# A residual stream with channels on the partitions, and full-height scores, in a two-layer trunk

## The chip, the cores and the metric

One core of a Trainium2 chip runs the whole program. The metric is device time in microseconds, the median of the runs shown. The engines are PE (TensorE, with its weight loads PEld), DVE (VectorE), ACT (ScalarE), POOL (GpSimd) and SP (SyncE, whose queue issues nearly all DMAs).

## The reference

512 tokens of 1024 channels go through two layers. Each layer normalises, projects, runs two groups of heads, gates them, projects back and adds to the residual x; then a per-layer embedding is added through a sigmoid gate. All arithmetic is float32.

```python
for i in range(2):
    h = rms_norm(x, norm_gain[i])
    y = even_layer(h) if i == 0 else odd_layer(h)
    x = x + y
    gate = sigmoid(rms_norm(x, ple_norm_gain[i]) @ w_ple_gate[i])
    x = x + (p[i] @ w_ple_proj[i]) * gate

def odd_layer(h):                      # layer 1
    cq, ck, cv, cg, dq, dk, dv, dg = split(h @ w_in)
    cq, ck, dq, dk = [rope(rms_norm(z, gain)) for z in ...]   # 8 heads of 64
    oc = dilated_attention(cq, ck, cv)       # head group C, causal patterns
    od = diff_attention(dq, dk, dv, lam)     # D: softmax 1 - lam * softmax 2
    return concat(oc * silu(cg), od * silu(dg)) @ w_out
```

Layer 0 has the same shape with head group A (each query attends to its 128 best keys by an indexer) and B (a window of 128 keys with sinks).

## The kernel before, in words

Tokens come in 4 tiles of 128 (NT), channels in 8 K tiles of 128 (NK). Every operand of a large product is split into a high and a low part in a reduced float32 format (`hilo`: ACT writes the high part, DVE the rest), and a product takes three matmuls, `PASSES = ((0, 0), (0, 1), (1, 0))`. The activations of the running projection lie in `AT`, channels on the partitions, [128, hi/lo, 8 K tiles, 512 tokens].

The residual `X` has tokens on the partitions. `norm` turns it: `turn` does 4 transposes on PE for each token tile and half of the channels and splits the result into AT, while `norm_scale` takes the sum of squares on ACT and a power on POOL, for a scale per token (`rs`). A scale per token is applied at evacuation, where tokens are partitions. Where they are columns (`proj_gate`), `scale_rows` sends the scales through DRAM and back to all partitions.

`proj_tok` computes a projection with tokens on the partitions, for 4 token tiles in 4 banks of PSUM (tag mm): order "kt" walks the K tiles outside, "tok" one bank after the other. `head_evac` scales, rotates and normalises the heads, turns them back with 4 transposes (tag tk), and `put_heads` writes [channels, tokens] in a pair of tiles (high, low). `put_stacked`, used in layer 0, instead stacks high and low parts of one head over 128 partitions by 4 DMAs, so that `scores` needs 2 matmuls for a head. In layer 1, `score_pairs` computes two heads at once in 64-row matmuls, 3 passes each, placed next to one another (`together`). The scores go to banks of tag sk, the attention output to tag ob. `out_half` adds the output projection to X, `ple` does the gate: tanh on ACT with the scale per token, and two DVE passes.

The order is that of a planner. `Program` records all calls (so every row of the profile has the line of the one place that issues them, L278) and `order()` schedules them per engine by a table of prices (`_price`, `LATENCY`) and by numbers (`LEADS`, one row for each kind of part) that move a part forwards or back in rank. The order on each engine is then fixed, SP included: a DMA that waits holds back those behind it. Rings set further waits: raw weights 4 tiles, split weights (w) 8, slots 8, mm banks 4, sk 2, tk 1, ob 1.

PE starts with ten products of zeros while the first loads are under way; x and the weights of the first projection come by K tiles 0, 1, then 2 and 3 of x in one load.

Of the kernel before, what the change touches and what calls it, by code (L numbers as in the profile page):

```python
# [12 lines left out]
F32 = mybir.dt.float32  # L13
# [18 lines left out]
    "att": (-392, -476, -265, 55, 575, -382, 44, 15, -6, -149, -341, -446, -4, -57, 63, -14, 2, 2, -287, 388, 0, 0,  # L32
         -65, 0, 0, -340, 0, -3, -78, 11, -243, 35, 122, -14, 0, -146),
    "ev": (12, 0, -121, 83, 78, -30, 61, -7, 7, 155, 29, 342, -212, 353, -715, 362, 407, -56, 322, -31, 200, 16, -145,
         -150, 0, 30, -1, -7, 53, -154, 6, 182, -674, -420, 817, -28, -108, -22, 70, -40, 70, 33, -1100, -2051, 35,
         822, 12, -44, 0, 0, -2, 0, 0, -147, 0, -27, -283, 17, 0, 12, 205, -6, 199, 0, -12, -29, 1, 69, -144, -2, 0,
         -60, -17, -132, -121, 0, -4, -30, -25, 158, -369, 425, 0, 348, 223, 189, -144, 392, -848, 105, -367, 17,
         -129, -1338, 5, 109, -567, -263, 0, -2347, -61, 293, 0, -2, 0, 1, -4, -10366, 101, 61, -322, 216, 72, 25,
         -1240, 202, 109, 0, 142, 0),
    "idx": (-5, -2, 0),  # L40
    "mm": (15, 0, 153, 0, 10, -336, -84, 2, 8, 4, 0, -30, 30, -5, 88, -12, -304, 0, 41, 13, 136, -25, 206, -141, -135,
         -6, -996, -1930, -2303, -10383),
    "norm": (-3, -2, 0, -170, 60, -38, 0, -13, 142, 15, 0, -227, 0, -49, 15, -1, 0, 0, -396, -7, 21, 0, 0, -1844),
    "rows": (0, 898),
    "ss": (-64, 0, 0, 340, 576, 4, -39, 1269, 0, 0, -74, 119, 196, 55, 333, 112, -4, 45, -250, -182, 70, 0, 0, 1, 14,
         -119, 0, 74, 0, 1, 0, -88),
    "tab": (279, 13, -4, 0, -137, -2),
    "top": (193, -101, -908, -1349, 180, 58, -8, -21, -2, 3, -1659, -1846),
    "w": (-57, 169, 413, -21, 0, -44, -172, 0, 3, 0, -2, 1, -44, 74, -2, -20, -89, 234, 3, 68, -363, 0, 0, -80, -19,
         0, -19, 0, -854, -1336),  # L50
    "x": (2, 0),
    "y": (825, 483, 0, -2, -20, 0, 0, -16, 32, 4, 0, 202, 1, -123, -517, -335),
    None: 62,
# [4 lines left out]
SWITCH = 200  # L58
WHOLE = frozenset(range(512))
PR = 8  # L60
QB = 2
# [18 lines left out]
class Program:  # L80
# [18 lines left out]
    def __init__(self, tc):  # L99
        self.tc = tc  # L100
        for e in self.ENGINES:
            setattr(self, e, _Engine(self, e))
        self.calls, self.cost, self.after, self.rank = [], [], [], []
        self.lead, self.parts = LEADS.get(None, 0), {}
        self.touched, self.users, self.rings, self.bytes, self.groups = {}, {}, {}, {}, {}
        self.mode, self.joined, self.place, self.extra = {}, None, 0, {}
# [23 lines left out]
    def _price(self, engine, method, reads, writes):  # L130
# [22 lines left out]
        return 218 / 128 * n  # L153

    @contextmanager
    def together(self):

        self.joined = []
        yield
        i, = set(self.joined)  # L160
        self.cost[i] /= 2
        self.joined = None

    def add(self, engine, method, args, kw):
        if self.joined:
            i = self.joined[0]
            self.calls[i][1].append((method, args, kw))
        else:
            i = len(self.calls)
            self.calls.append((engine, [(method, args, kw)]))  # L170
            self.rank.append((self.place - self.lead, i))
            self.cost.append(0)
            self.after.append(set())
        self.place += 1
        if self.joined is not None:
            self.joined.append(i)
# [4 lines left out]
        if engine == "tensor":  # L181
            self.mode[i] = reads[0].ap[0][1], writes[0].ap[0][1]
# [43 lines left out]
    def order(self):  # L226
# [17 lines left out]
        dma, mode = 0.0, None  # L244
# [4 lines left out]
        while len(out) < n:  # L249
# [6 lines left out]
            if i in self.mode:  # L256
                t += SWITCH * (mode not in (None, self.mode[i]))
                mode = self.mode[i]
# [23 lines left out]
def tile_trunk(ctx: ExitStack, tc: tile.TileContext, a: dict, out: bass.AP):  # L282
# [38 lines left out]
    for _ in range(10):  # L321
        nc.tensor.matmul(bank, zeros[:, :P], zeros, start=True, stop=True)
# [83 lines left out]
    def proj_tok(pieces_n, evac, tiles=range(NT), order="kt", act=None, swap=0, cut=False, first=False):  # L406
# [5 lines left out]
        def mms(t, i, c0=0, c1=n, passes=range(3)):  # L412
            kt, w2 = pieces[i]
            for c in passes:
                xa, wa = PASSES[c]
                nc.tensor.matmul(banks[t][:, c0:c1], act[kt ^ (4 * swap)][:, xa, t * P:(t + 1) * P], w2[:, wa, c0:c1],
                                 start=(i == 0 and c == 0), stop=(i == last and c == 2))
        if order == "kt":
# [10 lines left out]
            for t in tiles:  # L429
                evacuate(evac, t, banks[t])  # L430
        else:
            for t in tiles:
                halves = ((0, 256), (256, 512)) if cut and t == NT - 1 else ((0, n),)
                for c0, c1 in halves:
                    banks[t] = mm_bank()
                    for i in range(last + 1):
                        mms(t, i, c0, c1)
                    evacuate(evac, t, banks[t], *((c0, c1) if cut else ()))

    @nc.part("mm")  # L440
    def proj_gate(pieces_n, y0, done, rsb):
# [3 lines left out]
        for i, (kt, w2) in enumerate(pieces):  # L445
            for m in range(4):
                for c, (xa, wa) in enumerate(PASSES):
                    nc.tensor.matmul(banks[m], w2[:, wa, m * P:(m + 1) * P], AT[:, xa, kt, :],
# [34 lines left out]
    def norm_scale(t, rs, times=1.0):  # L483
# [5 lines left out]
        if times != 1.0:  # L489
# [640 lines left out]
```

## Time and profile before

| what | us |
|---|---|
| median of 3 runs | 676.76 (676.32 to 677.66) |
| profiled execution, its own time | 677.39 |
| its span, first to last instruction | 675.6 |
| PE busy | 668.0 (99%) |
| DVE busy | 513.7 (76%) |
| ACT busy | 415.4 (61%) |
| POOL busy | 68.7 (10%) |
| mean DMA rate | 110 GB/s |

The mean granted TensorE clock over the span is 1.00. Matmuls overlap in PE, so the length of one is more than what it costs in a row; pace is read from start to start. A tile's name in a row is that of the program without its number: `sk<-ident,slot` is a transpose of the residual, `sk<-slot,slot` a score, `mm<-w,AT` or `mm<-AT,w` a projection (what streams stands first, then what is stationary). A form such as 64*128 64x512 gives the rows and columns of the array that are used, then the shape that streams.

### The profile page before, as it was taken

How to read it: one execution, taken by the hardware profiler on the slowest of the kernel's cores; microseconds unless marked ns; L12 is line 12 of the kernel's file. 1: busy time of each engine (PE TensorE's matmuls, PEld its weight loads, DVE VectorE, ACT ScalarE, POOL GpSimd, SP SyncE). 2: the span in 40 equal slices, each digit the busy share in tenths (PEclk: the TensorE clock that was granted, in tenths of full speed). 3: DMA queues.
4: the chain of work that ended last, by engine and by line, in shares of the span. 5: the costliest groups of instructions: out<-in, count | busy, mean ns of one | idle time of the engine just before them, and what ended most of it. 6: DMA issues, size and time to landing. Idle time of an engine off the chain costs nothing.

```text
span 675.6 us, 10378 instructions
## 1 busy us (share of the span) xinstructions
PE 668.0 (99%) x3494; PEld 543.9 (81%) x3494; DVE 513.7 (76%) x1225; ACT 415.4 (61%) x957; POOL 68.7 (10%) x55
## 2 busy tenths in 40 slices
PE   8999999999999999999999999999999999999997
PEld 5888888888988888887778877777887777888886
DVE  6699999999999646464795298989869698655443
ACT  6765678999889725355554365766637476564341
POOL 0120132000100000000230040003031000100100
PEclk9999999999999999999999999999999999999999
DMA  9855146653131521253353322123213034132222
GB/s 333 299 144 153 63 126 168 183 148 141 48 111 49 185 79 54 71 183 101 87 156 99 94 62 79 48 63 94 86 40 97 29 114 136 48 111 63 93 79 78
DMA packets 49621, 74.23 MB, mean 110 GB/s; under 512 B 5920, under 2 KB 18592, under 8 KB 49312
## 3 DMA queue, kind: packets, MB, share of 16 engines
q1 hardware_dynamic: 49424, 73.56, 35.3%
q8 instruction: 27, 0.44, 0.3%
q14 instruction: 26, 0.21, 0.1%
q10 hardware_dynamic: 144, 0.02, 0.0%
HBM read 61.49 MB, written 6.30 MB: 100 GB/s over the span
## 4 chain that ended last, share of the span: by engine, by line
PE 92%; DMA 3%; DVE 2%; ACT 1%; issue 1%; SPq 0%; DVEq 0%; ACTq 0%
PE mm L278 70%; PE sk L278 8%; PE ob L278 7%; PE tk L278 6%; DMA raw<-in_w_in_odd_dram 2%; DMA slot<-in_xT_dram 1%; DVE t L278 1%; DMA raw<-in_w_out_odd_dram 1%; DVE w L278 1%; ACT w L278 0%; DVE AT L278 0%; ACT t L278 0%; DVE slot L278 0%; SPq L278 0%; DVE tiny L278 0%
## 5 line engine op out<-in xcount | busy, mean ns | idle before, releaser
L278 PE MATMUL mm<-w,AT 128*128 128x512 f32 (+2 forms) x1728 | 433.6, 397 | 1.2 <-ACT w L278 0.6
L278 PEld LDWEIGHTS mm<-w,AT 128*128 128x128 f32 x1728 | 313.4, 188 | 69.6 <-issue 1.6
L278 PE MATMUL mm<-AT,w 128*128 128x512 f32 x384 | 104.9, 404 | 0.0
L278 ACT ACTIVATE w<-raw,gains 128x512 fp32r<-128x512 f32 x96 | 67.7, 722 | 58.8 <-PE mm L278 51.5
L278 DVE SCALAR_TENSOR_TENSOR w<-raw,gains,w 128x512 fp32r<-128x512 f32 x96 | 69.9, 746 | 39.1 <-ACT w L278 38.7
L278 POOL TENSOR_TENSOR tiny<-tiny,mhalf 128x8 f32<-128x8 f32 (+1 forms) x32 | 56.9, 1780 | 351.2 <-DVE tiny L278 351.2
L278 PEld LDWEIGHTS mm<-AT,w 128*128 128x128 f32 x384 | 68.6, 189 | 12.9 <-issue 1.1
L278 ACT ACTIVATE pr<-pr,nm 128x256 f32<-128x256 f32 (+3 forms) x128 | 68.6, 539 | 11.6 <-DVE nm L278 11.3
L278 PE MATMUL sk<-slot,slot 128*128 128x256 f32 (+7 forms) x368 | 64.6, 330 | 0.0
L278 DVE TENSOR_TENSOR w<-raw,w 128x512 fp32r<-128x512 f32 x80 | 53.8, 682 | 14.0 <-ACT w L278 13.6
L278 ACT CAST w<-raw 128x512 fp32r<-128x512 f32 x79 | 47.6, 620 | 22.2 <-PE mm L278 13.4
L278 PEld LDWEIGHTS sk<-slot,slot 64*128 64x128 f32 (+1 forms) x368 | 43.9, 187 | 12.0 <-issue 3.8
L278 PE MATMUL tk<-ident,pr 128*128 128x128 f32 x256 | 43.7, 275 | 0.0
L278 DVE SCALAR_TENSOR_TENSOR t<-t,slot 128x512 f32<-128x512 f32 (+1 forms) x17 | 11.2, 659 | 35.0 <-ACT t L278 35.0
L278 PEld LDWEIGHTS ob<-pt,Ve 128*128 128x128 f32 x272 | 35.1, 191 | 2.7 <-ACT pt L278 1.2
L278 PE MATMUL ob<-pt,Ve 128*128 128x128 f32 x272 | 37.2, 276 | 0.0
L278 PEld LDWEIGHTS tk<-ident,pr 128*128 128x128 f32 x256 | 31.2, 141 | 7.0 <-ACT pt L278 1.5
L278 ACT ACTIVATE t<-mm,rsn 128x512 f32<-128x512 f32 (+1 forms) x17 | 11.0, 662 | 40.0 <-PE mm L278 40.0
L278 DVE TENSOR_TENSOR t<-raww,tab 128x512 f32<-128x512 f32 x48 | 32.4, 684 | 4.0 <-ACT raww L278 3.9
L278 DVE CUSTOM_DVE_ANT_0 pr<-sk,cpack 128x128 f32<-128x128 f32 (+3 forms) x72 | 31.1, 461 | 5.6 <-PE sk L278 5.5
L278 ACT COPY pt<-tk 128x512 f32<-128x512 f32 (+3 forms) x56 | 27.4, 489 | 12.1 <-PE tk L278 8.6
L278 POOL TENSOR_TENSOR rsn<-tiny,mhalf 128x1 f32<-128x1 f32 x16 | 11.3, 710 | 215.6 <-DVE tiny L278 215.5
(100 smaller groups left out, 797.1 us busy)
## 6 DMA issues: line engine op xcount, KB each, us to landing
raw<-in_w_in_odd_dram SPq DMA_DIRECT2D x64, 256.0 KB, 2.8
raw<-in_w_in_even_dram SPq DMA_DIRECT2D x36, 256.0 KB, 3.0
raw<-in_w_ple_gate_dram SPq DMA_DIRECT2D x32, 256.0 KB, 2.6
slot<-in_x_dram SPq DMA_DIRECT2D x16, 256.0 KB, 6.6
raw<-in_w_out_even_dram SPq DMA_DIRECT2D x16, 256.0 KB, 2.8
raw<-in_w_out_odd_dram SPq DMA_DIRECT2D x16, 256.0 KB, 2.6
slot<-qh SPq DMA_DIRECT2D x22, 128.0 KB, 2.4
slot<-ql SPq DMA_DIRECT2D x22, 128.0 KB, 2.5
```

The source lines that it names most:

```text
L278: getattr(getattr(nc, engine), method)(*args, **kw)
```

## The change

The residual X now has channels on the partitions. The residual is loaded from the transposed copy of x that the host passes already, the output projection, the embedding product and the gate swap their stationary and moving operand (`flip`), and the result is written as (channels, tokens) and turned on the host. `norm` has no transposes: `split_x` splits each K tile from SBUF into AT, `add_squares` squares it on ACT and adds the squares up on DVE, `column_scales` sums over the partitions with 4 float32 matmuls against a column of −0.5 and takes one power on POOL, and `scale_rows` makes rows of the scales by 4 transposes and a copy, without DRAM. The gate's evacuation multiplies by these rows on DVE ahead of tanh. Gates and ck take a new order "mix".

For C and D, keys are stacked as in layer 0 (`put_stacked`), and queries go to DRAM (`put_far`) and are fetched for each score by `fetch`, twice high and low over 64 partitions, into a ring of three tiles (`HOMES`). The scores are 128-row matmuls, 2 for each head. The first loads of x come as K tiles 0, 1, 2, 3 one at a time with the weights in turn, and nine products of zeros stand in place of ten. The planner loses its price for changes of form, and its numbers LEADS are new, all of them.

```diff
-    "norm": (-3, -2, 0, -170, 60, -38, 0, -13, 142, 15, 0, -227, 0, -49, 15, -1, 0, 0, -396, -7, 21, 0, 0, -1844),
+    "norm": (-7, -21, -1139, -422, 0, 163, 0, -1317, 0, -65, -255, 143, -554, 273, -6, 8, -797, 9, 343, 0, 45, 356,
...
-SWITCH = 200
...
+HOMES = ("ve", "acc12", "acc3")
...
-    for _ in range(10):
+    for _ in range(9):
...
-                nc.tensor.matmul(banks[t][:, c0:c1], act[kt ^ (4 * swap)][:, xa, t * P:(t + 1) * P], w2[:, wa, c0:c1],
-                                 start=(i == 0 and c == 0), stop=(i == last and c == 2))
+                x2, mine = act[kt ^ (4 * swap)], slice(t * P, (t + 1) * P)
+                if flip:
+                    nc.tensor.matmul(banks[t][:, c0:c1], w2[:, wa, mine], x2[:, xa, c0:c1],
+                                     start=(i == 0 and c == 0), stop=(i == last and c == 2))
+                else:
+                    nc.tensor.matmul(banks[t][:, c0:c1], x2[:, xa, mine], w2[:, wa, c0:c1],
+                                     start=(i == 0 and c == 0), stop=(i == last and c == 2))
         if order == "kt":
...
+        elif order == "mix":
+            early = [t for t in tiles if not (cut and t == NT - 1)]
+            for t in early:
+                banks[t] = mm_bank()
+            for i in range(4):
+                for t in early:
+                    mms(t, i)
+            for t in early:
+                for i in range(4, last + 1):
+                    mms(t, i)
+                evacuate(evac, t, banks[t])
...
     def scale_rows(rs):
+
+        b = t_bank()
+        for t in range(NT):
+            nc.tensor.transpose(b[:, t * P:(t + 1) * P], rs[:, t:t + 1].to_broadcast([P, P]), ident)
         rows = sb.tile([P, T], F32, name=uid("rows"), tag="rows", bufs=1)
-        line = dram.tile([NT, P], F32, name=uid("line"), tag=uid("line"), bufs=1)
-        nc.sync.dma_start(out=line.rearrange("t p -> p t"), in_=rs)
-        nc.sync.dma_start(out=rows, in_=line.rearrange("t p -> (t p)").partition_broadcast(P))
+        nc.scalar.copy(out=rows, in_=b)
         return rows
 
     @nc.part("norm")
-    def turn(t, half, to):
-        b = s_bank()
-        for i in range(4):
-            nc.tensor.transpose(b[:, i * P:(i + 1) * P], X[half][:, t, i * P:(i + 1) * P], ident)
-        hs = slice(to * 4, to * 4 + 4)
-        bv = b.rearrange("p (k n) -> p k n", k=4)
-        hilo(AT[:, 0, hs, t * P:(t + 1) * P], AT[:, 1, hs, t * P:(t + 1) * P], bv)
+    def split_x(k, to):
+        hilo(AT[:, 0, to, :], AT[:, 1, to, :], X[k // 4][:, k % 4, :])
+
+    @nc.part("ss")
+    def add_squares(acc, k):
+        sq = acc if k == 0 else tmp()
+        nc.scalar.activation(out=sq, in_=X[k // 4][:, k % 4, :], func=AF.Square, scale=1.0 / 32.0)
+        if k:
+            nc.vector.tensor_tensor(out=acc, in0=acc, in1=sq, op=ALU.add)
+
+    @nc.part("rs")
+    def column_scales(acc, times):
+        b = t_bank()
+        for t in range(NT):
+            nc.tensor.matmul(b[:, t:t + 1], acc[:, t * P:(t + 1) * P], mhalf[:, :1], start=True, stop=True)
+        e = tiny(4)
+        nc.vector.tensor_scalar(out=e, in0=b[:, :NT], scalar1=-2.0 * times ** -2, scalar2=EPS * times ** -2,
+                                op0=ALU.mult, op1=ALU.add)
+        rs = sb.tile([P, NT], F32, name=uid("rsn"), tag="rsn", bufs=2)
+        nc.gpsimd.tensor_tensor(out=rs, in0=e, in1=mhalf[:, :NT], op=ALU.pow)
+        return rs
 
     def norm(times=1.0, swap=0):
-        rs = sb.tile([P, NT], F32, name=uid("rsn"), tag="rsn", bufs=2)
-        for t in range(NT):
-            for half in range(2):
-                turn(t, half, half ^ swap)
-            norm_scale(t, rs, times)
-        return rs
+
+        acc = sb.tile([P, T], F32, name=uid("qh"), tag="qh", bufs=QB)
+        for k in range(NK):
+            split_x(k, k ^ (4 * swap))
+            add_squares(acc, k)
+        rs = column_scales(acc, times)
+        return rs, scale_rows(rs)
...
+    def put_far(dst, t, bank):
+
+        hi, lo = [sb.tile([P, 4, P], F32R, name=uid(x), tag=x, bufs=QB) for x in ("qh", "ql")]
+        hilo(hi, lo, bank.rearrange("p (k n) -> p k n", k=4))
+        home = dram.tile([2, P, 4, P], F32, name=uid("far"), tag=uid("far"), bufs=1)
+        for c, part in enumerate((hi, lo)):
+            nc.sync.dma_start(out=home[c], in_=part.bitcast(F32))
+        dst[t] = home
...
+    fetched = [0]
+
+    def fetch(far, p, qb):
+
+        n = fetched[0] = fetched[0] + 1
+        q = sb.tile([P, 2, 2, P], F32R, name=uid("q"), tag=HOMES[n % len(HOMES)], bufs=1)
+        for u in range(2):
+            nc.sync.dma_start(out=q[64 * u:64 * u + 64].bitcast(F32),
+                              in_=far[qb][:, :, p, :].rearrange("c (j d) n -> d c j n", j=2))
+        return q
+
+    def score_pairs(far, kT, wants):
 
         banks = [s_bank(), s_bank()]
-        found, o = [], 0
+        found, o = {}, 0
         for p, qb in reversed(wants):
             n = (qb + 1) * P
-            found.append((p, qb, o, n))
+            q = fetch(far, p, qb)
+            for j, bank in enumerate(banks):
+                for c in range(2):
+                    nc.tensor.matmul(bank[:, o:o + n], q[:, c, j, :], kT[j][:, p, :n], start=c == 0, stop=c == 1)
+            found[p, qb] = [bank[:, o:o + n] for bank in banks]
             o += n
-        found.reverse()
-        with nc.together():
-            for p, qb, o, n in found[::-1]:
-                for c, (qa, ka) in enumerate(PASSES):
-                    for j, bank in enumerate(banks):
-                        rows = slice(64 * j, 64 * j + 64)
-                        nc.tensor.matmul(bank[:, o:o + n], qT[qa][rows, p, qb * P:(qb + 1) * P],
-                                         kT[ka][rows, p, :n], start=c == 0, stop=c == 2)
-        return {(p, qb): [bank[:, o:o + n] for bank in banks] for p, qb, o, n in found}
+        return {w: found[w] for w in wants}
...
-                nc.scalar.activation(out=th, in_=bank[:, c0:c1], func=AF.Tanh, scale=rs[:, t:t + 1])
+                nc.vector.tensor_tensor(out=th, in0=bank[:, c0:c1], in1=rows[:, c0:c1], op=ALU.mult)
+                nc.scalar.activation(out=th, in_=th, func=AF.Tanh)
                 nc.vector.scalar_tensor_tensor(out=th, in0=th, scalar=1.0, in1=pw[:, t, c0:c1],
                                                op0=ALU.add, op1=ALU.mult)
                 xs = X[c][:, t, c0:c1]
                 nc.vector.scalar_tensor_tensor(out=xs, in0=th, scalar=0.5, in1=xs, op0=ALU.mult, op1=ALU.add)
-                nc.sync.dma_start(out=out[0, t * P:(t + 1) * P, c * 512 + c0:c * 512 + c1] if last else xkept[c][:, t, :], in_=xs)
-            proj_tok(w, evac, order="tok", swap=swap, cut=last and c == 1)
+                k = 4 * c + t
+                nc.sync.dma_start(out=out[k * P:(k + 1) * P, c0:c1] if last else xkept[c][:, t, :], in_=xs)
+            proj_tok(w, evac, order="mix", swap=swap, cut=last and c == 1, flip=True)
...
-    for k0, k1 in ((1, 2), (2, 4)):
+    for k0, k1 in ((1, 2), (2, 3), (3, 4)):
...
-    reload_x(x_in)
+    reload_x(lambda t, c: a["xT"][(4 * c + t) * P:(4 * c + t + 1) * P, :])
-    ple(0, pw0, norm(0.5, 1), False, 1)
-    rs1 = norm()
+    ple(0, pw0, norm(0.5, 1)[1], False, 1)
+    rs1, rows1 = norm(1.0, 1)
...
-    proj_tok(weights(ocols("ck"), range(NK), 2), head_evac(ckT, (tab_ck[:, 0], tab_ck[:, 1]), rs1), order="tok")
+    proj_tok(weights(ocols("ck"), range(NK), 2), head_evac(ckT, (tab_ck[:, 0], tab_ck[:, 1]), rs1, put=put_stacked), order="mix", swap=1)
...
-    proj_tok(wcq, head_evac(cqT, (tab_cq[:, 0], tab_cq[:, 1]), rs1))
+    proj_tok(wcq, head_evac(cqT, (tab_cq[:, 0], tab_cq[:, 1]), rs1, put=put_far), swap=1)
-    proj_tok(wdk, head_evac(dkT, (tab_dk[:, 0], tab_dk[:, 1]), rs1))
+    proj_tok(wdk, head_evac(dkT, (tab_dk[:, 0], tab_dk[:, 1]), rs1, put=put_stacked), swap=1)
-    proj_tok(wdq, head_evac(dqT, (tab_dq[:, 0], tab_dq[:, 1]), rs1))
+    proj_tok(wdq, head_evac(dqT, (tab_dq[:, 0], tab_dq[:, 1]), rs1, put=put_far), swap=1)
...
-    out = nc.dram_tensor("out_0_dram", (1, T, D), F32, kind="ExternalOutput").ap()
+    out = nc.dram_tensor("out_0_dram", (D, T), F32, kind="ExternalOutput").ap()
-    return r.results[0]["out_0_dram"]
+    return np.ascontiguousarray(r.results[0]["out_0_dram"].T)[None]
```

SP at the start of the program; the name in front of the arrow is the tile that is filled (slot_76 is x, raw the weights). Before:

```order
L278 DMA slot_76<-in_xT_dram 128x512
L278 DMA raw_80<-in_w_in_even_dram 128x512
L278 DMA slot_76<-in_xT_dram 128x512
L278 DMA raw_81<-in_w_in_even_dram 128x512
L278 DMA slot_76<-in_xT_dram 128x2x512
L278 DMA raw_82<-in_w_in_even_dram 128x512
L278 DMA raw_83<-in_w_in_even_dram 128x512
L278 DMA slot_77<-in_xT_dram 128x2x512
L278 DMA slot_79<-in_w_in_even_dram 128x2x512
L278 DMA slot_77<-in_xT_dram 128x2x512
```

After:

```order
L259 DMA slot_76<-in_xT_dram 128x512
L259 DMA raw_80<-in_w_in_even_dram 128x512
L259 DMA slot_76<-in_xT_dram 128x512
L259 DMA raw_81<-in_w_in_even_dram 128x512
L259 DMA slot_76<-in_xT_dram 128x512
L259 DMA raw_82<-in_w_in_even_dram 128x512
L259 DMA slot_76<-in_xT_dram 128x512
L259 DMA raw_83<-in_w_in_even_dram 128x512
L259 DMA slot_77<-in_xT_dram 128x2x512
L259 DMA slot_79<-in_w_in_even_dram 128x2x512
L259 DMA slot_77<-in_xT_dram 128x2x512
L259 DMA slot_79<-in_w_in_even_dram 128x2x512
```

The load of K tiles 2 and 3 of x has become two, each ahead of the weights of its own K tile.

PE at the end of the first layer, where the last gate products give way to the first products of layer 1 (mm_959 and mm_934 to mm_937 are banks; w split weights; AT the activations). Before:

```order
L278 MATMUL mm_959<-w_952,AT 128x512
L278 MATMUL sk_922<-ident,slot_784 128x128
L278 MATMUL mm_959<-w_952,AT 128x512
L278 MATMUL sk_922<-ident,slot_784 128x128
L278 MATMUL sk_928<-ident,slot_784 128x128
L278 MATMUL mm_959<-w_952,AT 128x512
L278 MATMUL sk_922<-ident,slot_784 128x128
L278 MATMUL sk_928<-ident,slot_784 128x128
L278 MATMUL mm_959<-w_954,AT 128x512
L278 MATMUL sk_922<-ident,slot_784 128x128
L278 MATMUL sk_928<-ident,slot_784 128x128
L278 MATMUL mm_959<-w_954,AT 128x512
```

After, the products with K tile 3 of ck, between them the column sums (tk<-mhalf,qh):

```order
L259 MATMUL mm_934<-w_925,AT 128x512 x2
L259 MATMUL tk_904<-mhalf,qh_896 128x1 x4
L259 MATMUL mm_934<-w_925,AT 128x512
L259 MATMUL mm_935<-w_925,AT 128x512 x3
L259 MATMUL mm_936<-w_925,AT 128x512 x3
L259 MATMUL mm_937<-w_925,AT 128x512 x3
L259 MATMUL mm_934<-w_927,AT 128x512 x3
L259 MATMUL mm_934<-w_929,AT 128x512 x3
L259 MATMUL mm_934<-w_931,AT 128x512 x3
L259 MATMUL mm_934<-w_933,AT 128x512 x3
L259 MATMUL mm_935<-w_927,AT 128x512 x3
L259 MATMUL mm_935<-w_929,AT 128x512 x3
```

The transposes of X between the products are gone; four narrow matmuls stand after 38 products of ck, and the products walk K tiles 4 to 7 bank by bank.

PE in head group C, the scores. Before (slot_941 and slot_942 are the high and low queries, slot_1038 and slot_1039 the keys):

```order
L278 MATMUL sk_1099<-slot_941,slot_1038 128x384
L278 MATMUL sk_1100<-slot_941,slot_1038 128x384
L278 MATMUL sk_1099<-slot_942,slot_1038 128x384
L278 MATMUL sk_1100<-slot_942,slot_1038 128x384
L278 MATMUL sk_1099<-slot_941,slot_1039 128x384
L278 MATMUL sk_1100<-slot_941,slot_1039 128x384
L278 MATMUL mm_1153<-AT,w_1089 128x512 x3
L278 MATMUL mm_1150<-AT,w_1091 128x512 x2
L278 MATMUL sk_1103<-slot_941,slot_1038 128x512
L278 MATMUL sk_1104<-slot_941,slot_1038 128x512
L278 MATMUL sk_1103<-slot_942,slot_1038 128x512
L278 MATMUL sk_1104<-slot_942,slot_1038 128x512
```

After (q is a fetched tile; slot_916 and slot_917 are the stacked keys of the two heads). Three rows above these stand the last scores from q_1089, with two products behind them, and q_1121 is the next to use its home:

```order
L259 MATMUL mm_1245<-w_1172,AT 128x512 x2
L259 MATMUL sk_1092<-slot_916,q_1094 128x384 x2
L259 MATMUL sk_1093<-slot_917,q_1094 128x384 x2
L259 MATMUL mm_1151<-AT,w_1082 128x512
L259 MATMUL mm_1245<-w_1172,AT 128x512
L259 MATMUL mm_1152<-AT,w_1082 128x512
L259 MATMUL sk_1097<-slot_916,q_1099 128x512 x2
L259 MATMUL sk_1098<-slot_917,q_1099 128x512 x2
L259 MATMUL mm_1246<-w_1172,AT 128x512
L259 MATMUL mm_1152<-AT,w_1082 128x512
L259 MATMUL mm_1246<-w_1172,AT 128x512
L259 MATMUL sk_1119<-slot_916,q_1121 128x256 x2
```

The two columns of pairs, three passes of each, have become two matmuls for a head, and between the scores stand products of other parts.

SP in the same stretch of the new program (far is a query tile in DRAM, raw a weight tile); before, there were only weight loads:

```order
L259 DMA q_1099<-far_1066 64x4x128 x2
L259 DMA far_1033<-ql_1032 128x512
L259 DMA raw_1293<-in_w_in_odd_dram 128x512
L259 DMA q_1089<-far_1033 64x4x128 x2
L259 DMA q_1121<-far_1044 64x4x128 x2
L259 DMA q_1122<-far_1033 64x4x128 x2
L259 DMA q_1127<-far_1055 64x4x128 x2
L259 DMA q_1132<-far_1066 64x4x128 x2
L259 DMA q_1221<-far_1055 64x4x128 x2
L259 DMA q_1215<-far_1044 64x4x128 x2
L259 DMA raw_1295<-in_w_in_odd_dram 128x512
L259 DMA raw_1297<-in_w_in_odd_dram 128x512
```

Seven fetches, two DMAs each, stand one after the other ahead of the next weight loads.

## Rows read from the trace of the kernel before

**Rows 1.** The page, part 1: engine, busy us, share of the span, instructions.
```profile
PE 668.0 (99%) x3494; PEld 543.9 (81%) x3494; DVE 513.7 (76%) x1225; ACT 415.4 (61%) x957; POOL 68.7 (10%) x55
```

**Rows 2.** The page, part 4: the chain that ended last, by engine.
```profile
PE 92%; DMA 3%; DVE 2%; ACT 1%; issue 1%; SPq 0%; DVEq 0%; ACTq 0%
```

**Rows 3.** Waits of PE: us in total, times, longest us.
```profile
PE ob L278 <- DVE zeros L278: 1.2, 1, 1.2
PE ob L278 <- ACT pt L278: 0.8, 1, 0.8
```

**Rows 4.** Timeline of PE, four stretches: start us, length us, instruction [idle before <-releaser].
```profile
53.32 0.28 PE L278 MATMUL sk<-slot,slot 128*128 128x256 f32 x1
53.44 0.39 PE L278 MATMUL mm<-w,AT 128*128 128x512 f32 x1
...
77.83 1.13 PE L278 MATMUL sk<-slot,slot 128*128 128x512 f32 x4
...
219.81 1.05 PE L278 MATMUL ob<-pt,Ve 128*128 128x128 f32 x8
...
290.10 1.03 PE L278 MATMUL sk<-ident,slot 128*128 128x128 f32 x8
290.89 9.37 PE L278 MATMUL mm<-w,AT 128*128 128x512 f32 x39
```

**Rows 5.** Groups of PE by form: busy us, mean ns of one | idle before.
```profile
L278 PE MATMUL sk<-ident,slot 128*128 128x128 f32 x96 | 17.8, 272 | 0.2 <-DVE AT L278 0.2
```

**Rows 6.** Timeline of PE, 411 to 416.5 us (scores of C).
```profile
411.02 0.80 PE L278 MATMUL sk<-slot,slot 64*128 64x384 f32 x6
411.75 1.43 PE L278 MATMUL mm<-AT,w 128*128 128x512 f32 x5
413.11 0.97 PE L278 MATMUL sk<-slot,slot 64*128 64x512 f32 x6
414.00 1.66 PE L278 MATMUL mm<-AT,w 128*128 128x512 f32 x6
415.59 0.91 PE L278 MATMUL sk<-slot,slot 64*128 64x256 f32 x12
416.43 0.51 PE L278 MATMUL mm<-AT,w 128*128 128x512 f32 x1
```

**Rows 7.** Timeline of PE, ACT, DVE and SP, 0 to 16 us, five rows.
```profile
10.70 0.50 PE L278 MATMUL mm<-w,AT 128*128 128x512 f32 x1 [0.64 <-ACT w L278]
11.63 4.70 PE L278 MATMUL mm<-w,AT 128*128 128x512 f32 x19 [0.43 <-DVE w L278]
...
8.80 1.34 ACT L278 ACTIVATE AT<-slot,gains 128x512 fp32r<-128x512 f32 x2 [2.01 <-DMA slot<-in_xT_dram]
...
13.49 1.29 DVE L278 TENSOR_TENSOR w<-slot,w 128x512 fp32r<-128x512 f32 x2
...
2.59 0.43 SPq L278 DMA_DIRECT2D slot<-in_xT_dram  x1
```

**Rows 8.** DMA issues: transfer, queue, count, KB each, median us to landing.
```profile
slot<-in_xT_dram SPq DMA_DIRECT2D x2, 256.0 KB, 3.0
```

**Rows 9.** Timeline of DVE, the first of its last two passes.
```profile
671.89 0.43 DVE L278 SCALAR_TENSOR_TENSOR t<-t,slot 128x256 f32<-128x256 f32 x1 [1.83 <-ACT t L278]
```

**Rows 10.** Timeline of DVE at the first layer end, back to back.
```profile
320.12 0.68 DVE L278 TENSOR_TENSOR AT<-sk,AT 128x512 fp32r<-128x512 f32 x1
320.72 0.68 DVE L278 SCALAR_TENSOR_TENSOR slot<-t,slot 128x512 f32<-128x512 f32 x1
```

**Rows 11.** Windows: length, busy PE PEld DVE ACT POOL, clock, DMA share, GB/s.
```profile
314.00:335.00 21.00, 20.82 (x102) 16.35 (x101) 13.64 (x26) 11.43 (x24) 4.91 (x4) 1.00 0.45 122
335.00:350.00 15.00, 14.89 (x73) 11.78 (x72) 13.85 (x24) 9.77 (x18) 3.97 (x2) 1.00 0.47 128
```

**Rows 12.** Tile qh on SP: issue ns min/median/max, and landing.
```profile
L278 SPq DMA_DIRECT2D slot<-qh x22: 590/604/805, 33.2 to 185.7; - x22
...
DMA to landing us min/median/max: 2.4/2.4/6.1
```

## What I predict of the change

> **What bounds the kernel now.** I read the busy table first [rows 1]: TensorE (PE) is busy 99% of the span. The chain of waits agrees: 92% of the way to the last instruction is PE's own work [rows 2]. The two longest waits of PE by name are 1.2 and 0.8 us [rows 3]. So almost every instruction that leaves or joins PE's queue should show in the time, at its pace from start to start (matmuls overlap, so a row's mean of 400 ns is not its cost), and work on the other engines shows only where it makes PE wait.
>
> The paces come from the timeline of PE: the length of a run less the last one's own length, over the rest. 39 wide products of 512 columns take 9.37: (9.37 − .40) / 38 = .235 each. Eight records of 128 columns take 1.05, the last one .28: .11 each [rows 4]. These eight are float32 matmuls, which leave two records each, so one such matmul costs .22.
>
> **The change, part by part.** All terms are for the profiled execution, 677.39 us (span 675.6 and 1.79 around it); it stands .63 above the median of 676.76.
>
> 1. *The transposes of the norm go.* 96 of them, .27 long [rows 5]; eight in 1.03 [rows 4], so (1.03 − .27) / 7 = .109 each, −10.5. To the start of the wide product behind them those eight take .79, .099 each: low bound −9.5. Nothing on PE stands in for them where the activations are made: the residual now lies with channels on the partitions, and ACT and DVE split it straight from SBUF.
>
> 2. *Row scales by transposes.* scale_rows is called four times, 4 transposes each: 16 × .109 = +1.7. The DRAM round trips that they replace (4 DMAs) stood off PE's chain and give nothing.
>
> 3. *Column sums.* Three norms with 4 float32 matmuls each, one column wide, with a full stationary operand. No row shows one column. The nearest are 128 columns at .11 a record and 256 columns at .12 (53.32 to 53.44) [rows 4]: half the columns there save next to nothing, so I take .11 a record, 12 × 2 × .11 = +2.6; if the pair of records costs as one, +1.3. A price that only a page gives: the Trainium skill (TensorEngine Tiling (Array Packing), section Instruction Overhead) gives a matmul of one column the latency of one of 60. As an estimate from that page, 60 cycles at 2.4 GHz make 24 records 0.6 us and the sum 2.0 lower; no row here has so few columns.
>
> 4. *Scores of C and D.* Before, 24 groups of 64-row matmuls (six wide, or twelve narrow), side by side in pairs. From 411.02 to 416.43 three groups stand with 11 wide products: 5.41 − 11 × .235 = 2.82, .94 a group, with the step in and out of the form; from their own starts to the next start they take .73, .89 and .84 [rows 6]. So 24 groups are 19.7 to 22.6; I take 22, with which all PE instructions at their paces add up to the span. After, 128 full-height matmuls, 32 of each width. Layer 0 has such scores: 512 columns (1.13 − .40) / 3 = .243, 256 columns .12, 128 columns .11 [rows 4], and 384 between them, .18. 32 × (.243 + .18 + .12 + .11) = 20.9. So −1.1, between +1.2 and −1.7.
>
> Here a rule speaks against the change. By the rows six matmuls of 512 columns in 64 rows take .89, so a pair side by side .30, where one alone costs .243: a gain of 1.6 and not of 2 [rows 4, 6]. The Trainium skill (TensorEngine Tiling (Array Packing), sections Theoretical Speedup and Key Properties) gives up to 2× for a contraction of 64 rows and a drain at each change of mode. At the full 2× a pair would cost as one: 24 × (.243 + .18 + .12 + .11) = 15.7 before, so the edit would add 5.2 and the whole change give 1.4. The trace shows less than 2×, and .05 to .1 for the step.
>
> 5. *Zeros and the first loads.* PE stops ahead of 10.70 and of 11.63 for K tile 2 of x and the weights [rows 7]. The load of x of 128x2x512 is issued at 2.59, and ACT's split waits for it until 8.80 [rows 7]. Cut in two, with the weights in turn, K tile 2 has half the bytes ahead of it; 256 KB of x took 3.0 us at the median [rows 8], so I put it ready near 8.5. PE comes to it at 9.3 (one zero less takes .4 off 9.7). The stops, 1.5 by the gaps between starts, and the zero would give 1.9, until the next limit: K tile 4's low part, the first of two passes from 13.49, is done at 13.49 + .6 = 14.1 [rows 7], where PE would be at 13.8. So −1.6; between 0 (the transfers share the same engines, and K tile 2 is no earlier) and −2.0.
>
> 6. *Tail.* After the last product come ACT, two DVE passes and the store. DVE now multiplies by the row scales ahead of ACT: one more pass of 128x256, .43 [rows 9]: +.45.
>
> 7. *DVE and ACT.* DVE gets 21 additions and 17 multiplies of 512 columns. Back to back its passes start .60 apart [rows 10], so 23 us on an engine busy 514 of 676 [rows 1]. Most lie at the two ends of the gates, where DVE is busy 13.64 of 21.00 and 13.85 of 15.00 [rows 11]. The cover is PE's queue: gates and ck now walk four K tiles over four banks, 48 × .235 = 11.3 us, before they want the later K tiles, and the column sums stand behind 38 of these products, 8.9 us after the last gate product. The chain of the last channel tile is multiply .6, tanh .7, two passes 1.2, split 1.2, square .7, addition .6, with latencies some 6, and about 2 of backlog: 8. I put +.3 on it, bounds 0 and 2. Without the cover PE stops at the column sums with all that is behind them.
>
> 8. *The fetches of q.* 32 of C and D, two DMAs each, on SP: a new wait, since they go into a ring of three tiles, and the fourth waits for the scores of the first. Behind a waiting fetch on SP stand weight loads (raw), and PE waits for both. The nearest rows are the 22 stores slot<-qh of 128 KB: .60 to issue, landing 2.4 at the median and 6.1 at most [rows 12]. A tile is back some .1 + .6 + 2.4 = 3.1 after its last score, 6.8 at the worst. PE's work in between, by the order and the paces, is 10 × .235 + 4 × .18 + 4 × .243 = 4.0 for q_1089 to q_1121; 12 of 29 reuses have 3.7 to 7.0, the rest 8 to 57. At 3.1 all are covered; I put +.3, bounds 0 and 4.
>
> The loads of weights and of x that only move keep their number and size; SP waits for its turn more than it issues, and I cost them at nothing. POOL has three powers where it had twelve, off the chain.
>
> Sum: −10.5 + 1.7 + 2.6 − 1.1 − 1.6 + .45 + .3 + .3 = −7.85. 677.39 − 7.85 = 669.5 own time, 668.9 against the median.
>
> **Rivals.**
> (a) *The ring of q binds: slower.* For it: twelve gaps under 7.1 and seven fetches in a row ahead of the next weight load on SP. If every reuse needed 6.8, the shortfalls (gaps 3.7, 3.7, 4.0, 4.0, 4.3, 4.4, 4.4, 4.9, 6.1, 6.8, 6.8, 7.0) add up to 22. A stop in one gap lengthens those that overlap it, so half to all is real; all of it gives 691, half 680. It decides from a landing of about 5.4: the shortfalls are then 16, half of them 8, what the change saves. Against it: the median of 2.4 [rows 12]. 5%.
> (b) *Pairs at their full worth*, the rule in 4: −1.4 in all, 675.3. Against it the timed groups [rows 6]. 1%.
> (c) *DVE bounds the boundaries.* There 7 additions and 8 multiplies, 9 us, join 27.5 us of work in 36 [rows 11]; half of it late costs 4.5: 673.4. For it: 13.85 of 15.00. Against it: PE is busy 20.82 of 21.00 and 14.89 of 15.00 there now, behind a chain through transposes. 14%.
> (d) *The first loads bring nothing*, K tile 2 arrives no earlier: 670.5. 12%.
> (e) *The ends that favour it*: one record's price for the column sums (−1.3), a little off every other term (−1.5): 666. 13%.
> The forecast, 668.9 with 667 to 671 of its own: 55%.
>
> **How the numbers follow.** What can be told from no change here is 0.2%, 1.35 us: faster lies under 675.4, slower over 678.1. The forecast, (c), (d) and (e) are all faster. The range runs from a little under (e), 664.8, to past (c) and short of (a), 675; it leaves out (a), (b) and the outer parts of (c) and (e), some 14 in 100, and the rest for what I have not seen. Faster .92; within 0.2% .04 (the mild end of (a), half of (b), the far end of (c)); slower .04 (the rest of (a)).
>
> **What would show it.** PE busy near 660 with no row of sk<-ident; 24 records of tk<-mhalf at a pitch near .11 (half of it says (e)); scores sk<-slot,q at the paces of layer 0; no stop of PE at 9.7 and a short one near 13.8 at K tile 4 (a stop at K tile 2 says (d)). Waits of PE for q, or for weights whose load SP issued behind a fetch, say (a); waits for AT, rows or the column sums at a layer's end say (c). I am wrong if the fetches land later than 5.4, or if PE stands still for over 3 us in all after 20 us.

## The result

The changed kernel takes 665.75 us (664.71 to 666.45, four runs) against 676.54 before (676.32 to 677.66): the ratio is 0.9836, 95% interval [0.9819, 0.9853], 10.8 us less. The forecast was 668.9, in a range of 664.8 to 675.0: right in direction and range, with some 3 us of gain that no term of the sum had.

The profiled execution takes 664.71, span 662.8. The page of the changed kernel, part 1 (engine, busy us, share, instructions), and the chain of part 4:

```profile
PE 654.7 (99%) x3373; PEld 543.9 (82%) x3373; DVE 530.0 (80%) x1246; ACT 415.1 (63%) x937; POOL 63.4 (10%) x46
...
PE 88%; DVE 5%; DMA 3%; issue 1%; ACT 1%; POOL 0%; SPq 0%; DVEq 0%
```

Against [rows 1, 2] PE has 13.3 us less to do, where the span fell by 12.8, and still bounds; DVE has 16.3 more, and its share of the chain went from 2% to 5%. The two profiles (664.71 and 677.39) are further apart than the medians. The waits of PE (us in total, times, longest):

```profile
PE ob L259 <- DVE zeros L259: 1.2, 1, 1.2
PE sk L259 <- DMA q<-far: 0.5, 2, 0.3
PE mm L259 <- DVE w L259: 0.5, 2, 0.2
PE ob L259 <- ACT pt L259: 0.4, 1, 0.4
PE mm L259 <- ACT raww L259: 0.4, 1, 0.4
PE sk L259 <- issue: 0.3, 1, 0.3
```

Against [rows 3] the new wait is the one for the fetches of q. No row of sk<-ident is left [rows 5]. The new groups, by form:

```profile
L259 PE MATMUL sk<-slot,q 128*128 128x512 f32 x32 | 10.7, 414 | 0.0
L259 PE MATMUL sk<-slot,q 128*128 128x384 f32 x32 | 8.1, 358 | 0.0
L259 PE MATMUL sk<-slot,q 128*128 128x256 f32 x32 | 5.9, 295 | 0.3 <-issue 0.3
L259 PE MATMUL sk<-slot,q 128*128 128x128 f32 x32 | 4.8, 276 | 0.5 <-DMA q<-far 0.5
L259 PE MATMUL tk<-ident,rsn 128*128 128x128 f32 x16 | 3.2, 272 | 0.0
L259 PE MATMUL tk<-mhalf,qh 128*128 128x1 f32 x24 | 3.2, 218 | 0.0
```

The timeline of PE at the column sums of the first gate's norm (start us, length us, instruction):

```profile
277.24 0.28 PE L259 MATMUL tk<-mhalf,qh 128*128 128x1 f32 x2
277.38 0.48 PE L259 MATMUL mm<-AT,w 128*128 128x512 f32 x1
277.70 0.28 PE L259 MATMUL tk<-mhalf,qh 128*128 128x1 f32 x2
277.83 0.47 PE L259 MATMUL mm<-AT,w 128*128 128x512 f32 x1
278.15 0.28 PE L259 MATMUL tk<-mhalf,qh 128*128 128x1 f32 x2
278.29 0.47 PE L259 MATMUL mm<-AT,w 128*128 128x512 f32 x1
278.60 0.28 PE L259 MATMUL tk<-mhalf,qh 128*128 128x1 f32 x2
```

Three sums and three products take 1.36 from start to start; three products alone take .69, so a sum costs .22, and no stop of PE is marked ahead of it. By the Trainium skill (TensorEngine Tiling (Array Packing), section Instruction Overhead) the 24 records would have been some 0.6 us, an estimate; the trace says 2.6.

### The profile page after: what moved, and what is told of

Its sections match the earlier page's. It is cut to its first block, busy times and chain, and to the rows that moved or that the text cites. A ratio compares the mean times of both kernels' runs of the same rounds, so it can differ in the third digit from the quotient of the medians.

```text
span 662.8 us, 10361 instructions
## 1 busy us (share of the span) xinstructions
PE 654.7 (99%) x3373; PEld 543.9 (82%) x3373; DVE 530.0 (80%) x1246; ACT 415.1 (63%) x937; POOL 63.4 (10%) x46
## 4 chain that ended last, share of the span: by engine, by line
PE 88%; DVE 5%; DMA 3%; issue 1%; ACT 1%; POOL 0%; SPq 0%; DVEq 0%
PE mm L259 68%; PE ob L259 7%; PE tk L259 7%; PE sk L259 6%; DMA raw<-in_w_in_even_dram 1%; DVE t L259 1%; DMA q<-far 1%; DVE w L259 1%; DVE acc L259 1%; DVE few L259 1%; DMA raw<-in_w_ple_proj_dram 1%; POOL tiny L259 0%; SPq L259 0%; DMA far<-ql 0%; ACT w L259 0%
## 5 line engine op out<-in xcount | busy, mean ns | idle before, releaser
L259 PE MATMUL mm<-AT,w 128*128 128x512 f32 (+1 forms) x1176 | 291.0, 393 | 0.0
L259 PEld LDWEIGHTS mm<-AT,w 128*128 128x128 f32 x1176 | 212.6, 188 | 40.4 <-ACT t L259 0.2
L259 PE MATMUL mm<-w,AT 128*128 128x512 f32 (+1 forms) x936 | 238.7, 398 | 0.5 <-DVE w L259 0.5
L259 PEld LDWEIGHTS mm<-w,AT 128*128 128x128 f32 x936 | 170.4, 188 | 35.4 <-ACT AT L259 0.7
L259 PE MATMUL sk<-slot,slot 128*128 128x256 f32 (+3 forms) x176 | 41.3, 323 | 0.0
L259 ACT ACTIVATE t<-t 128x512 f32<-128x512 f32 (+1 forms) x33 | 20.2, 615 | 31.0 <-DVE t L259 31.0
L259 DVE TENSOR_TENSOR t<-mm,rows 128x512 f32<-128x512 f32 (+1 forms) x33 | 22.1, 670 | 14.5 <-PE mm L259 9.7
L259 PEld LDWEIGHTS sk<-slot,slot 128*128 128x128 f32 x176 | 28.7, 189 | 4.9 <-ACT t L259 1.0
L259 DVE TENSOR_TENSOR AT<-slot,AT 128x512 fp32r<-128x512 f32 x40 | 26.9, 686 | 5.3 <-PE mm L259 3.1
```

Of the source, the lines that this page charges most:

```text
L259: getattr(getattr(nc, engine), method)(*args, **kw)
```

## The experiments

Each kernel was timed beside the kernel before in five rounds. Differences from the changed kernel are those of the ratios, times 676; the intervals of the two ratios together make them uncertain by 1.3 to 1.9 us.

**The changed kernel again.**

> The changed kernel once more, beside its variants. Every theory: 665.7, within 0.7.

665.97, ratio 0.9850 [0.9835, 0.9865]. This run left a second profile of the changed kernel (666.60, span 664.7), in which DVE has 10% of the chain:

```profile
PE 656.1 (99%) x3373; PEld 545.4 (82%) x3373; DVE 530.3 (80%) x1246; ACT 415.8 (63%) x937; POOL 61.6 (9%) x46
```

**1. Transposes put back.** 32 ahead of the column sums of each norm:

```diff
             nc.tensor.matmul(b[:, t:t + 1], acc[:, t * P:(t + 1) * P], mhalf[:, :1], start=True, stop=True)
+            if t == 0:
+                nc.calls[-1][1][:0] = [("transpose", (b[:, i % 4 * P:i % 4 * P + P], ident, ident), {}) for i in range(32)]
```

> The changed kernel with 96 transposes put back: 32 of ident directly ahead of the column sums of each of the three norms, into the bank that these overwrite; the order of everything else is the same. The prediction's step 1 (0.109 each, all on PE's path): +10.5 on 665.9, 676.4; if they fill the stops ahead of the column sums (0.56, 0.36, 0.56) 674.9. Rival, the transposes were never on the path: 666 to 668.

677.38, ratio 1.0014 [1.0001, 1.0027]: +11.1. This one part takes the whole gain away. The timeline of PE in this kernel:

```profile
278.10 3.66 PE L259 MATMUL tk<-ident 128*128 128x128 f32 x32
281.59 0.28 PE L259 MATMUL tk<-mhalf,qh 128*128 128x1 f32 x2
```

3.49 for 32 is .109 each, the price of the prediction, with nothing hidden. Here they stand in one run; between products, where the old ones stood, a transpose costs the same, as the row scales show further down.

**2. Column sums twice.**

```diff
             nc.tensor.matmul(b[:, t:t + 1], acc[:, t * P:(t + 1) * P], mhalf[:, :1], start=True, stop=True)
+            nc.calls[-1][1].append(nc.calls[-1][1][0])
```

> The changed kernel with each of the 12 column sums issued twice. Step 3 of the prediction (0.22 each): +2.6, 668.5. The pair of records as one (0.11): +1.3, 667.2. No cost beside the stops ahead of them: 665.9.

669.15, ratio 0.9894 [0.9875, 0.9913]: +3.0. Two records a sum at .11 each (+2.6); the price as one lies at the edge of what the interval allows, and the timeline above excludes it.

**3. Scores in 64 rows again.** The fetches stay, all those of a bank ahead of its scores; two heads are computed side by side as before:

```diff
-            q = fetch(far, p, qb)
-            for j, bank in enumerate(banks):
-                for c in range(2):
-                    nc.tensor.matmul(bank[:, o:o + n], q[:, c, j, :], kT[j][:, p, :n], start=c == 0, stop=c == 1)
...
+        qs = [fetch(far, p, qb) for p, qb in reversed(wants)]
+        with nc.together():
...
+                for i, c in enumerate((0, 0, 1)):
+                    for j, bank in enumerate(banks):
+                        rows = slice(64 * j, 64 * j + 64)
+                        nc.tensor.matmul(bank[:, o:o + n], q[rows, c, j, :], kT[j][rows, p, :n], start=i == 0, stop=i == 2)
```

> The changed kernel with the scores of C and D in 64-row matmuls again, two heads side by side, three passes, 24 groups; fetches of q stay (the low part of the keys is left out, the high part is used twice). Prediction's step (22 against 20.9): 666.8. Theory that the groups cost more than their own length, 24.7 by the stretches around them against 21.7: +3.0, 668.7. Pairs at their full worth (15.7): 660.5.

665.88, ratio 0.9855 [0.9831, 0.9879]: +0.3, no difference. The page of this kernel, part 1, and its waits of PE, all of them:

```profile
PE 656.8 (99%) x3437; PEld 539.1 (81%) x3437; DVE 532.4 (80%) x1246; ACT 414.7 (63%) x937; POOL 61.0 (9%) x46
```

```profile
PE ob L274 <- DVE zeros L274: 1.2, 1, 1.2
PE mm L274 <- DVE w L274: 0.2, 1, 0.2
```

In the first profile of the changed kernel PE is busy 2.1 less, in the second 0.7 less, but it waits for q, .5 in the first; in the second that wait is

```profile
PE sk L259 <- DMA q<-far: 2.2, 4, 1.1
```

So full-height scores save .7 to 2.1 us of PE's work, and the waits for q, which the 64-row kernel does not show, give some or all of it back. With an uncertainty of 1.9 the time cannot tell the prediction's +0.9 from nothing; it excludes the +3.0 of the longer groups and pairs at their full worth (660.5).

**4. First loads of x as a pair.**

```diff
-    for k0, k1 in ((1, 2), (2, 3), (3, 4)):
+    for k0, k1 in ((1, 2), (2, 4)):
```

> The changed kernel with K tiles 2 and 3 of x in one load again; nine zeros stay. The prediction's step 5: +1.6, 667.5. From the stops that the trace of the changed kernel still shows in its first 20 us (0.7 against 1.9 before): +1.2, 667.1. Rival, K tile 2 is no later: 665.9, within 0.5.

666.34, ratio 0.9847 [0.9829, 0.9864]: −0.2, no difference. The timeline of ACT, the split of K tiles 2 and 3 in this kernel:

```profile
7.72 1.34 ACT L259 ACTIVATE AT<-slot,gains 128x512 fp32r<-128x512 f32 x2 [0.65 <-DMA slot<-in_xT_dram]
```

With the same pair of transfers it starts at 7.72, not at 8.80 [rows 7]. The kernel before, in experiment 6, has the same loads as [rows 7] and starts there at 7.78; its PE runs through:

```profile
5.07 12.22 PE L278 MATMUL mm<-w,AT 128*128 128x512 f32 x47
```

**5. The flip taken back.** The swap of stationary and moving operand in the output projection, the embedding product and the gates:

```diff
-                     act=[w2 for _, w2 in pT], flip=True)
+                     act=[w2 for _, w2 in pT])
...
-            proj_tok(w, add_x(c), order="kt" if c == 0 else order, flip=True)
+            proj_tok(w, add_x(c), order="kt" if c == 0 else order)
...
-            proj_tok(w, evac, order="mix", swap=swap, cut=last and c == 1, flip=True)
+            proj_tok(w, evac, order="mix", swap=swap, cut=last and c == 1)
```

> The changed kernel with stationary and moving operand as before in the output projection, the embedding product and the gates (so these products are not turned and the output is not the reference's); nothing else moves. Pace theory: the 744 products go from 0.2294 back to 0.2333 each, +2.9, the 48 of 256 columns give 0.2 back: 668.4, between 667.7 and 669.1. Rival, the pace difference comes from what runs beside: no change, 665.0 to 666.4.

667.84, ratio 0.9876 [0.9861, 0.9890]: +1.8. The timeline of PE at the gates, the changed kernel first, then this one:

```profile
282.63 30.25 PE L259 MATMUL mm<-AT,w 128*128 128x512 f32 x131
```

```profile
282.72 39.67 PE L259 MATMUL mm<-w,AT 128*128 128x512 f32 x169
```

(30.25 − .39) / 130 = .2297 with AT moving, (39.67 − .40) / 168 = .2338 with AT stationary. 744 products at .004 are 3.0, 0.2 of it given back by the 48 narrow ones; the time shows 1.8 of 2.8, within its uncertainty.

**6. Where AT lies.** In both kernels AT starts 64 bytes past a multiple of 512 in its partition, and the split weights start on one. Moving a small constant behind AT and another ahead of it shifts it by 64 bytes; the instructions and their order stay. The changed kernel:

```diff
-    gains = const.tile([P, 4, NK], F32, name="gains")
...
+    sink = const.tile([P, 2, 8], F32, name="sink")
...
     AT = const.tile([P, 2, NK, T], F32R, name="AT")
+    gains = const.tile([P, 4, NK], F32, name="gains")
...
-    sink = const.tile([P, 2, 8], F32, name="sink")
```

> The changed kernel with the activations AT starting 64 bytes earlier, on a multiple of 512 bytes as the split weights do; order and instructions are the same. Address theory: products with AT stationary go from 0.2333 to 0.2294, 936 of them, -3.6: 662.1. Role theory (which operand is stationary, not where it lies): no change, 665.0 to 666.4.

661.66, ratio 0.9796 [0.9779, 0.9812]: −3.7. The same runs of products, first in the changed kernel, then here:

```profile
330.31 13.32 PE L259 MATMUL mm<-w,AT 128*128 128x512 f32 x56
```

```profile
281.57 29.98 PE L259 MATMUL mm<-AT,w 128*128 128x512 f32 x131
...
328.76 12.97 PE L259 MATMUL mm<-w,AT 128*128 128x512 f32 x56
```

With AT stationary (13.32 − .40) / 55 = .235 becomes .2285; with AT moving .2297 becomes .2276. So it is the place of the tile, and in products of 512 columns the stationary operand feels it three times as much. Most of what experiment 5 took back is the same effect: with AT on a multiple of 512 the two roles differ by .0009, some 0.7 for 744 products (an estimate), in place of .004 and 3.0.

The same edit in the kernel before:

> The kernel before, with the activations AT starting 64 bytes earlier, on a multiple of 512 bytes; same instructions and order. Address theory: 1584 products with AT stationary go from 0.2333 to 0.2267 (-10.5), 384 with AT moving from 0.2300 to 0.2275 (-1.0), the 96 of 456 columns by -0.6: 675.9 - 12 = 664. Rival, the pace of the changed kernel depends on its own order: 675 to 677.

671.83, ratio 0.9930 [0.9912, 0.9948]: 4.7 faster, not 12. The timeline of PE, a run of 99 products, in the kernel before and here:

```profile
290.89 23.36 PE L278 MATMUL mm<-w,AT 128*128 128x512 f32 x99
```

```profile
288.43 22.77 PE L278 MATMUL mm<-w,AT 128*128 128x512 f32 x99
```

.2343 becomes .2283, as expected in kind; I had priced every product by the best pace (.2267), which only the quiet stretches reach. All 1584 together are busy 407.5 before and 401.1 here, 6.4 less where 10.5 were priced. And narrower products do not gain, though they have the same stationary tile; before, then here:

```profile
L278 PE MATMUL mm<-w,AT 128*128 128x456 f32 x96 | 21.0, 372 | 0.0
L278 PE MATMUL mm<-w,AT 128*128 128x256 f32 x48 | 5.6, 276 | 0.0
```

```profile
L278 PE MATMUL mm<-w,AT 128*128 128x456 f32 x96 | 21.1, 373 | 0.0
L278 PE MATMUL mm<-w,AT 128*128 128x256 f32 x48 | 5.9, 283 | 0.0
```

The spans of the two profiles differ by 7.0, of which the better landing of the first loads is a part.

All slots, the constants cpack and ident and the pr rows on multiples of 512 as well:

```diff
+    warm = tiny(8)
     zeros = sb.tile([P, 512], BF16, name="zeros", tag="pr", bufs=PR)
...
-    nc.scalar.activation(out=tiny(8), in_=mhalf, func=AF.Tanh)
+    nc.scalar.activation(out=warm, in_=mhalf, func=AF.Tanh)
```

(and vpack, mhalf and sink ahead of cpack, gains behind AT)

> The changed kernel with AT, the constants, the slots (heads, keys, values) and the rows pr all on multiples of 512 bytes; same instructions and order. If a score of 512 columns goes from 0.243 to 0.227 and the others in proportion, 303 of them: 661.7 - 2.5 = 659.2. If only AT and the weights count: 661.7, within 0.7.

662.40, ratio 0.9788 [0.9768, 0.9808]: the same as with AT alone. The slots, which started on 256 past a multiple of 512, gain nothing. The homes of q, stationary in the scores of C and D, stay 64 or 320 past one, so for those scores nothing is tested.

AT on a multiple of 128 (only sink moved ahead of it):

> The changed kernel with AT 64 bytes later: on a multiple of 128 bytes, not of 256 or 512. If 128 bytes are enough: as with 512, products with AT stationary at 0.2267, 661.9, within 0.8. If it takes 256 or 512: 0.2333 as in the changed kernel, 665.9, within 0.7.

667.23, ratio 0.9870 [0.9853, 0.9886]: not faster than the changed kernel; 128 bytes are not enough. The same two runs:

```profile
283.11 30.67 PE L259 MATMUL mm<-AT,w 128*128 128x512 f32 x131
...
331.18 13.28 PE L259 MATMUL mm<-w,AT 128*128 128x512 f32 x56
```

With AT stationary .234, as at 64; with AT moving .233, worse than at 64.

**7. Two homes for q.**

```diff
-HOMES = ("ve", "acc12", "acc3")
+HOMES = ("ve", "acc12")
```

> The changed kernel with two homes for q in place of three. A fetch is two issues of 0.6 and a landing of 3.0, 4.3 after its last score with the step between; by the order and the paces the gaps of the three homes fall short of that by 1.9 in all, of the two homes by 6.3. Ring theory: +2.2 to +4.4, 668 to 670. Rival, the waits for q come from the order of SP's queue and not from the ring: 665 to 667.

669.82, ratio 0.9901 [0.9885, 0.9917]: +3.4, in the range of the ring theory. But the planner orders some scores anew, and the profile (668.16) names less for q than the second one of the changed kernel, and more for pt:

```profile
PE ob L259 <- ACT pt L259: 1.7, 3, 0.8
PE sk L259 <- DMA q<-far: 1.4, 3, 0.7
```

So how much of the 3.4 is the ring and how much the new order is not shown.

**8. Fetches of q on POOL's queue**, with AT as in 6:

```diff
-            nc.sync.dma_start(out=q[64 * u:64 * u + 64].bitcast(F32),
+            nc.gpsimd.dma_start(out=q[64 * u:64 * u + 64].bitcast(F32),
```

> The changed kernel with AT on a multiple of 512 bytes and the fetches of q on POOL's queue in place of SP's. If the waits for q (1.1 to 2.2) come from what stands ahead of the fetches on SP: 661.9 - 1.5 = 660.4. If from the ring and the landing: 661.9, within 0.7. If POOL issues them more slowly: 663 to 668.

662.34, ratio 0.9797 [0.9780, 0.9814]: no gain over 661.66. No wait of PE for q is named by its profile any more, but waits for pt (0.9) and a wait put down to issue at a score (0.6) stand in its place.

## Why the prediction was right, and where it was not

Step 1 (the transposes, −10.5) carries the result: put back, they cost 11.1, at .109 each. Step 3 (column sums, +2.6) holds in the time and in the timeline. Step 2 (+1.7) was not tried alone, but its price is in the timeline of the changed kernel. Four of its transposes, with one product between each two:

```profile
329.25 0.28 PE L259 MATMUL tk<-ident,rsn 128*128 128x128 f32 x1
...
330.28 0.27 PE L259 MATMUL tk<-ident,rsn 128*128 128x128 f32 x1
```

1.03 for three steps is .343 a step; less .235 for the product, a transpose costs .11.

Step 7 (DVE) was right in that the cover of PE's queue holds: no wait for AT, for the row scales or at the column sums is among PE's in either profile of the changed kernel. Rival (c) did not come, though DVE has 16 us more.

Step 6 (the tail) came nearly as priced: from the last product to the end it is 4.9 in place of 4.3, so .6 for .45. DVE and ACT after the last product, one pass more than before [rows 9]:

```profile
657.99 0.42 DVE L259 TENSOR_TENSOR t<-mm,rows 128x256 f32<-128x256 f32 x1 [1.03 <-PE mm L259]
658.45 0.42 ACT L259 ACTIVATE t<-t 128x256 f32<-128x256 f32 x1 [2.40 <-DVE t L259]
658.90 0.43 DVE L259 SCALAR_TENSOR_TENSOR t<-t,slot 128x256 f32<-128x256 f32 x1 [0.48 <-ACT t L259]
659.36 0.42 DVE L259 SCALAR_TENSOR_TENSOR slot<-t,slot 128x256 f32<-128x256 f32 x1
```

Step 5 (first loads, −1.6) failed. The step was "these stops go". The stops of [rows 7] belonged to one execution, in which the pair of K tiles came into use 1.0 to 1.1 us later than in two other profiles with the same pair. I read a landing of one execution as a property of the program. Rival (d) describes what happened; with it alone the sum would have been 670.5.

Steps 4 and 8 (scores −1.1, ring +.3) came out together at 0 within the uncertainty, but not for the reasons given. The waits for q are .5 and 2.2 in the two profiles, inside the bounds of step 8, and two things were wrong in it. The first is the time for which a home is away: I counted one issue of .6 and a landing of 2.4; a fetch is two issues, and the landing is 3.0 at the median:

```profile
L259 SPq DMA_DIRECT2D q<-far x64: 573/602/1419, 394.5 to 552.0; - x64
...
DMA to landing us min/median/max: 2.6/3.0/5.4
```

So 4.3 in place of 3.1, with seven gaps under or near it. The second is larger: step 8 looked only at homes that are used again, and put the first trip of a query through DRAM at nothing. The four waits for q in the second profile, in the timeline of PE:

```profile
398.74 0.71 PE L259 MATMUL sk<-slot,q 128*128 128x256 f32 x4 [0.47 <-DMA q<-far]
414.40 0.63 PE L259 MATMUL sk<-slot,q 128*128 128x128 f32 x4 [1.09 <-DMA q<-far]
419.45 0.49 PE L259 MATMUL sk<-slot,q 128*128 128x256 f32 x2 [0.41 <-DMA q<-far]
514.53 0.63 PE L259 MATMUL sk<-slot,q 128*128 128x128 f32 x4 [0.19 <-DMA q<-far]
```

The chain that ends at the second and the third of them has these transfers (start, length):

```profile
407.28 3.47 DMA far<-ql
...
411.45 2.82 DMA q<-far
...
415.69 3.62 DMA q<-far
```

The longest wait, 1.09, ends such a trip: the low part of the queries is stored from 407.28 on, and the fetch goes out when it has landed, at 410.75. In the first profile the longer of two waits, 0.3, ends the same trip. Only the third one here, .41, is the ring: its fetch goes out at 415.07, when the scores of the home's last user end, and is back 4.2 later. Of the others, .47 is for the first fetch of all, 4.4 on its way, and .19 for one whose two halves stand on SP with a store of other queries between them. So rival (a)'s mechanism was there, at under a tenth of its least price (11).

What the sum had not at all is the flip: 744 products change which operand is stationary, and I gave them the same pace. The trace of before has both kinds, and I took the pace from one of them. It is worth 1.8 by experiment 5 and 2.8 by the paces, and experiment 6 says that most of it is the place of AT.

Put together: −11.1 for the transposes, +3.0 for the sums, +1.7 (not tried alone) for the row scales, −0.3 for scores and fetches, −1.8 for the flip, +0.2 for the first loads and +.6 for the tail are −7.7, where 10.1 to 10.8 were measured. The zero that was dropped is not in this sum; PE's first product starts at 4.89 and 4.75 in the two profiles, 5.07 before. The rest, 2 to 3 us, is no more than the uncertainties of five differences together; whether it is one more effect stays open. The planner's new numbers, which order every part anew, were not tried alone and may hold some of it. The wait for pt of 0.8 [rows 3], which fell to 0.4, can only be a small part. PE is busy 654.7 and 656.1, where I had said near 660, so what the sum had not is work of PE, not a wait that went.

So the mechanism held in its largest term, and the nearness of the number is in part luck: a gain of 1.6 was priced that did not come, and some 4 us came that were not priced. The time is that of rival (e), 666, but not by its way, since its main term, one record's price for the column sums, is what the timeline excludes. In step 4, the whole change with pairs at their full worth should read −1.55, not −1.4; nothing hangs on it.

## What to carry to other kernels

Where one engine is busy 99% of the span, a sum of its instructions at their start-to-start paces gave the direction and the largest term of this change, and missed 3 of 11 us; put the part with the largest term back by itself to see that it is on the path. Take a separate pace for each role of the operands and look at where their tiles start: here a shift of 64 bytes gave 3.7 us for nothing, a third of what the whole change gave. A stop in the first ten microseconds of one profile is no property of the program until a second profile shows it, and a transfer made of several DMAs is late by the issue of all of them. Data that is sent through DRAM has two landings on its way, one for the store and one for the fetch; price both, not only the reuse of the tile that it is fetched into.

## What the runs showed of the hardware

A product of 512 columns took .2285 (AT stationary) and .2276 (AT moving) with both operands on multiples of 512 bytes, .235 with the stationary one 64 bytes past it, .234 with it 128 past, .2297 with the moving one 64 past and .233 with it 128 past. Products of 456 and 256 columns gained nothing from the multiple. Whether it is the multiple of 512 itself, or the same remainder as the other operand, no run tells apart; nor is a start 256 past it tried for AT. A float32 matmul of one column cost as much as one of 128 columns, .22, in two records of .11.
